# A row-wise logsumexp kernel: the bias of the first units as three one-row matmuls, and exp(bias) of the later stages made when they begin

## Chip, cores, metric

One core of a Trainium2 chip. The metric is the device time of one execution in microseconds (us), median of several executions; the profile page shows one of them. The profile's *span* is shorter than this time by about 1.8 us for the kernel before; that difference becomes part of the story.

## The reference

```python
def reference(x, bias):                    # x: 8 x 2048 x 2048 f32, bias: 8 x 256
    B, S, D = x.shape
    H = bias.shape[0]
    Dh = D // H
    x_heads = x.reshape(B, S, H, Dh).transpose(0, 2, 1, 3)
    x_heads = x_heads + bias[None, :, None, :]
    x_tiled = np.repeat(x_heads, 2, axis=2)
    mx = x_tiled.max(axis=-1, keepdims=True)
    return (mx.squeeze(-1) + np.log(np.exp(x_tiled - mx).sum(axis=-1))).astype(np.float32)
```

So 134 MB are read, and for each of 131,072 groups of 256 numbers one logarithm of a sum of exponentials is written twice.

## The kernel before

The rows are worked on in 64 units of 256 rows (2.097 MB each), in nine buffers `xt`. Units 0 to 53 are of one kind: PE adds the bias to heads 0 to 2 in PSUM (a bias matmul, then x times the identity), ACT takes exp; head 3 has exp on ACT and is multiplied by exp(bias) on DVE; heads 4 to 7 get the bias added on POOL, then exp on ACT; DVE sums heads 1 to 7, and ACT sums head 0 while it takes its exp. The last ten units use other divisions, which need more factors exp(bias). The parts that the change touches:

```python
    # bias as three bf16 parts that sum to the f32 value: made in one partition ...
    nc.gpsimd.tensor_copy(bparts[:, 0], bp)
    nc.gpsimd.tensor_sub(brest[:, 0], bp, bparts[:, 0])
    ...
    nc.gpsimd.tensor_copy(bparts[:, 2], brest[:, 1])
    # ... and gathered into three partitions, so that one matmul with 3 rows of ones adds all three
    for i in range(3):
        nc.gpsimd.dma_start(out=b3[i : i + 1, :], in_=bparts[:, i])
    ...
    for i, c in enumerate(range(G0, D, MM)):          # bias of heads 4 to 7, in all partitions
        spread(ps[i], c, c + MM)
        nc.vector.tensor_copy(b_rep[:, c - G0 : c - G0 + MM], ps[i])
    for c in range(W0, W2, MM):                       # factors exp(bias) of heads 3 to 6
        spread(w_ps[:, c - W0 : c - W0 + MM], c, c + MM)
    nc.scalar.activation(out=w_ps, in_=w_ps, func=ACT.Exp)
    nc.scalar.activation(out=w_sb, in_=b_rep[:, W1 - G0 :], func=ACT.Exp)
    ...
            for h, p in enumerate(got):               # the bias matmuls of one unit
                nc.tensor.matmul(p, lhsT=ones3, rhs=each_row(b3, h * Dh, Dh, K),
                                 start=True, stop=False)
    ...
            def pool_part(t=t, ...):                  # after a unit's sums: its buffer is loaded anew
                if add:
                    later(m, t, k0, k1, sums, add)
                if k1 == K and t + NBUF < T:
                    load(t + NBUF)
```

The softmax here doesn't subtract the row's maximum and nothing guards it: scores larger than these inputs give would overflow.

Of the kernel before, what the change touches and what calls it, by code (L numbers as in the profile page):

```python
# [11 lines left out]
ACT = mybir.ActivationFunctionType  # L12
# [2 lines left out]

K = 2
NBUF = 9

NWARM = 3

# [29 lines left out]
def kernel(  # L50
# [6 lines left out]
    nc = tc.nc  # L57
    P = nc.NUM_PARTITIONS
    B, S, D = x.shape
    H, Dh = bias.shape  # L60
# [5 lines left out]
    MM = 512  # L66


    V0, W0, G0, W1, W2 = Dh, 3 * Dh, 4 * Dh, 6 * Dh, 7 * Dh
# [7 lines left out]
    b_rep = sb.tile([P, D - G0], F32, name="b_rep")  # L77
    w_sb = sb.tile([P, D - W1], F32, name="w_sb")
    ident = sb.tile([P, P], F32, name="ident")
    ones = sb.tile([1, P], F32, name="ones")  # L80
    ones3 = sb.tile([3, P], BF16, name="ones3")
    b3 = sb.tile([3, CPE], BF16, name="b3")
    bparts = sb.tile([1, 3, CPE], BF16, name="bparts")
# [5 lines left out]
    res_last = sb.tile([P, P, 2], F32, name="res_last")  # L89
    xts = [sb.tile([P, K, D], F32, name=f"xt{i}") for i in range(NBUF)]  # L90
    w_ps = pp.tile([P, W2 - W0], F32, name="w_ps")


    one_ps = pp.tile([P, MM], F32, name="one_ps")
# [5 lines left out]
    def modes_of(t):  # L100
        return [modes for t0, modes in STAGES if t0 <= t][-1]

    def pieces(t):

        if len(modes_of(t)) == 1:
            return [(0, K, 0, D)]
        cols = [[(0, D)]] * K if t < T - 1 else LAST_COLS
        return [(k, k + 1, c0, c1) for k in range(K) for c0, c1 in cols[k]]

    def rows_of(t):  # L110

        b, blk = divmod(t, NBLK)
        v = x[b, blk * P * K : (blk + 1) * P * K, :]
        if b < B - 1:
            return v.rearrange("(p k) d -> p k d", k=K)
        return v.rearrange("(k p) d -> p k d", k=K)
# [5 lines left out]
    def on_x(t, ins, after):  # L122
        known = [u for u in users[t] if u.ins.engine != ins.ins.engine]
        for before in range(t % NBUF, t, NBUF):
            known += users[before]
# [12 lines left out]
    def load(t):  # L138
        after = last_uses[t - NBUF] if t >= NBUF else []
        for k0, k1, c0, c1 in pieces(t):  # L140
            loads[t, k0, c0] = on_x(
                t,
                nc.sync.dma_start(
                    out=xts[t % NBUF][:, k0:k1, c0:c1],
                    in_=rows_of(t)[:, k0:k1, c0:c1],
                ),
                after,
            )
# [14 lines left out]
    nc.scalar.dma_start(out=brow, in_=bias.rearrange("h j -> (h j)").unsqueeze(0))  # L163
    for t in range(NBUF):
        load(t)
# [9 lines left out]
    nc.gpsimd.tensor_sub(brest[:, 1], brest[:, 0], bparts[:, 1])  # L175
    nc.gpsimd.tensor_copy(bparts[:, 2], brest[:, 1])
    for i in range(3):
        nc.gpsimd.dma_start(out=b3[i : i + 1, :], in_=bparts[:, i])


    def spread(dst, c0, c1):
        nc.tensor.matmul(
            dst, lhsT=ones, rhs=brow[:, c0:c1], start=True, stop=True
        )

    for i, c in enumerate(range(G0, D, MM)):
        spread(ps[i], c, c + MM)
        nc.vector.tensor_copy(b_rep[:, c - G0 : c - G0 + MM], ps[i])
    for c in range(W0, W2, MM):
        spread(w_ps[:, c - W0 : c - W0 + MM], c, c + MM)  # L190
    nc.scalar.activation(out=w_ps, in_=w_ps, func=ACT.Exp)
    nc.scalar.activation(out=w_sb, in_=b_rep[:, W1 - G0 :], func=ACT.Exp)


    n_ps = [0]
# [4 lines left out]
    def on_bank(i, ins):  # L200
        for j, u in bank_users[i // 2]:
            if j != i and u.ins.engine != ins.ins.engine:
                tc.declare_no_dep(ins.ins, u.ins, reason="another bank")
        bank_users[i // 2].append((i, ins))
        return ins

    def put_bias(m, k0, k1):



        if m["late"]:
            pair = pairs[n_ps[0] % 2]
            n_ps[0] += 1
            got = [one_ps, pair[:, 0:MM], pair[:, MM : 2 * MM]]
            for h, p in enumerate(got):
                nc.tensor.matmul(  # L216
                    p,
                    lhsT=ones3,
                    rhs=each_row(b3, h * Dh, Dh, K),
                    start=True,  # L220
                    stop=False,
                )
            return got + [pair]
        n = m["pe"] * Dh
        rows = min(k1 - k0, max(MM // n, 1))
        got = []
        for k in range(k0, k1, rows):
            for c in range(0, n, MM):
                w = min(n - c, MM)
                bank = n_ps[0] % len(ps)  # L230
                p = ps[bank][:, 0 : rows * w]
                n_ps[0] += 1
                mm = nc.tensor.matmul(
                    p,
                    lhsT=ones3,
                    rhs=each_row(b3, c, w, rows),
                    start=True,
                    stop=False,
                )
                on_bank(bank, mm)  # L240
                got.append((k, k + rows, c, w, bank, p))
        return got

    def add_x(m, t, k0, c0, c1, got):
# [3 lines left out]
        for ka, kb, c, w, bank, p in got:  # L248
            if not c0 <= c < c1:
# [3 lines left out]
                lhsT=ident,  # L253
                rhs=xts[t % NBUF][:, ka:kb, c : c + w],
                start=False,
# [8 lines left out]
    def keep_warm():  # L264
        for _ in range(NWARM):
            nc.tensor.matmul(  # L266
                tps[B % 2][:, 0], lhsT=ident, rhs=ident, start=True, stop=True
            )
# [45 lines left out]
    def each_row(src, c, n, k_rows):  # L314

        return bass.AP(
            tensor=src.tensor,
            offset=src.offset + c,
            ap=[src.ap[0], [0, k_rows], [1, n]],
        )  # L320
# [124 lines left out]
    def sums_of(t):  # L445

        b, blk = divmod(t, NBLK)
        if b < B - 1:
            return R[b][:, :, :, blk]
        return R_last[:, :, blk, :].rearrange("p h k -> p k h")  # L450
# [20 lines left out]
    for t in range(T):  # L471
        xt = xts[t % NBUF]
        sums = sums_of(t)
        for k0, k1, c0, c1 in pieces(t):
            m = modes_of(t)[k0]
            add = None
            heads = []
            if c0 == 0:
                bias_here = bias_there
            if m["late"]:  # L480
                pe_part = late_heads(m, t, bias_here, sums)
            else:
                heads = add_x(m, t, k0, c0, c1, bias_here)

                def pe_part(t=t, heads=heads, sums=sums):
                    for k, h, bank, p, mm in heads:
                        sum_biased(t, k, h, bank, p, mm, sums)

            if c0 == 0:
                if next_units and not m["late"]:  # L490
                    bias_there = put_bias(*next_units.pop(0))
                if t > T_PROMPT and m["g0"] == H:
                    keep_warm()
                if m["g0"] < H:
                    add = g_add(m, t, k0, k1)
                if t < T - 1 or k0 == 0:
                    flush(for_pool)
            if t == T_PROMPT and c0 == 0:
                spread(one_ps, V0, W0)
                nc.scalar.activation(out=one_ps, in_=one_ps, func=ACT.Exp)  # L500
            h0 = max(c0 // Dh, m["pe"])
            h1 = min(c1 // Dh, m["g0"])
            hf = max(h0, min(h1, H - m["fold"]))
            if h0 < h1 and not m["late"]:
                done = exp_inplace(
                    t, xt[:, k0:k1, h0 * Dh : h1 * Dh], loads[t, k0, c0]
                )
                if hf < h1:
                    for_pool.append(fold(t, k0, hf, h1, sums, done))
            if c0 == 0:  # L510
                flush(for_pe)
            if not m["late"]:
                for k in range(k0, k1):
                    for h in range(h0, hf):
                        weigh(
                            t,
                            xt[:, k, h * Dh : (h + 1) * Dh],
                            h,
                            sums[:, k, h : h + 1],
                            done,  # L520
                        )

            def pool_part(t=t, m=m, k0=k0, k1=k1, sums=sums, add=add):
# [5 lines that stand above are left out]
            for_pool.append(pool_part)  # L529
            if m["g0"] < H:  # L530
                pe_part()
                if m["late"]:
                    bias_there = put_bias(*next_units.pop(0))
            elif heads:
                for_pe.append(pe_part)

        fb, at = divmod(t - 2, NBLK)
        if fb >= 0 and at == NBLK - 1:
            finish(fb)
            if fb == B - 2:  # L540
                store()
# [35 lines left out]
```

## Time and profile before

| | before |
|---|---|
| time, median (range) | 326.98 us (326.78 to 327.11) |
| span of the profiled run (its own time) | 325.4 us (327.16 us) |
| HBM read and written | 134.23 MB + 1.05 MB |

The page's views are quoted in the prediction below. How to read them: the slice rows are tenths of busy time in 40 equal slices; the chain follows the last instruction back to what released it; a timeline row is start, length, engine, line, what, with what ended the idle time in brackets.

### The profile page before, as it was taken

The numbers are of one execution on the slowest core, as the hardware profiler recorded it, in microseconds if no ns is written. First come the engines' busy times: TensorE is split into PE (matmuls) and PEld (weight loads), VectorE is DVE, ScalarE is ACT, GpSimd is POOL, SyncE is SP. The second block draws the span as 40 slices with busy tenths as digits, with TensorE's granted clock in tenths as the row PEclk, the third lists the DMA queues.
The fourth block names the chain that finished last, engine by engine and source line by source line (L and its number), as shares of the span: only waits on it lengthen the run. The fifth ranks groups of instructions, "written<-read, shape, count | busy, mean of one in ns | idle before, by whom it ended". The sixth has DMA issues, their size and how long they took to land.

```text
span 325.4 us, 2350 instructions
## 1 busy us (share of the span) xinstructions
PE 263.2 (81%) x649; PEld 98.6 (30%) x649; DVE 284.0 (87%) x306; ACT 264.7 (81%) x425; POOL 290.7 (89%) x123
## 2 busy tenths in 40 slices
PE   5398999599888789779779788887877897399984
PEld 2033333233323223223223223323223332044442
DVE  1008999999999999998998899989899799999985
ACT  1139999499969878987887969698788778889995
POOL 7999999899999999999999999999999899958874
PEclk9999999899979987997997979798998989569999
DMA  7999999999999999999999999999999999999995
GB/s 293 428 435 429 427 433 422 425 433 429 427 427 431 425 424 433 425 425 434 426 425 431 431 422 427 429 429 427 431 427 426 429 425 429 415 421 421 424 394 154
DMA packets 11934, 135.42 MB, mean 416 GB/s; under 512 B 1361, under 2 KB 1745, under 8 KB 2961
## 3 DMA queue, kind: packets, MB, share of 16 engines
q1 hardware_dynamic: 11824, 135.27, 98.9%
q8 instruction: 5, 0.08, 0.1%
q14 instruction: 7, 0.06, 0.0%
q0 software_dynamic: 96, 0.00, 0.0%
q10 hardware_dynamic: 2, 0.01, 0.0%
HBM read 134.23 MB, written 1.05 MB: 416 GB/s over the span
## 4 chain that ended last, share of the span: by engine, by line
DMA 48%; DVE 35%; POOL 6%; ACT 6%; PE 3%; issue 1%; SPq 0%; DVEq 0%
DMA xt<-in_x_dram 45%; DVE R L350 29%; ACT xt L331 5%; DVE xt L343 5%; POOL xt L325 4%; DMA b<-bparts 2%; PE pair L275 2%; DVE xt L366 2%; PE one_ps L275 1%; ACT xt L293 1%; DMA brow<-in_bias_dram 1%; POOL brest L173 1%; POOL brest L175 1%; PE pair L216 0%; POOL bparts L172 0%
## 5 line engine op out<-in xcount | busy, mean ns | idle before, releaser
L325 POOL TENSOR_TENSOR xt<-xt,b_rep 128x2048 f32<-128x2048 f32 x57 | 258.8, 4543 | 20.1 <-DMA xt<-in_x_dram 20.1
L350 DVE TENSOR_REDUCE R<-xt 128x14 f32<-128x3584 f32 (+1 forms) x56 | 214.5, 3831 | 1.9
L331 ACT ACTIVATE xt<-xt 128x2560 f32<-128x2560 f32 (+5 forms) x77 | 158.1, 2062 | 13.4 <-POOL xt L325 12.5
L275 PE MATMUL pair<-xt,ident 128*128 128x512 f32 x216 | 115.1, 660 | 0.0
L275 PE MATMUL one_ps<-xt,ident 128*128 128x512 f32 x108 | 66.7, 702 | 23.1 <-DMA xt<-in_x_dram 23.1
L293 ACT ACTIVATE xt<-pair 128x1024 f32<-128x1024 f32 x54 | 56.3, 1042 | 20.7 <-PE pair L275 19.3
L275 PEld LDWEIGHTS pair<-xt,ident 128*128 128x128 f32 x216 | 46.2, 214 | 61.5 <-issue 61.5
L343 DVE TENSOR_TENSOR xt<-xt,w_ps 128x512 f32<-128x512 f32 x54 | 36.8, 681 | 27.8 <-ACT xt L331 27.7
L286 ACT ACTIVATE xt<-one_ps 128x256 f32<-128x256 f32 x108 | 40.6, 391 | 7.9 <-PE one_ps L275 7.9
L216 PE MATMUL one_ps<-b,ones 3*128 3x512 bf16 x54 | 20.7, 383 | 18.4 <-ACT xt L286 12.4
L216 PEld LDWEIGHTS <-ones 3*128 3x128 bf16 x162 | 13.5, 92 | 70.2 <-issue 63.8
L216 PE MATMUL pair<-b,ones 3*128 3x512 bf16 x108 | 32.3, 378 | 0.0
L275 PEld LDWEIGHTS one_ps<-xt,ident 128*128 128x128 f32 x108 | 17.0, 198 | 46.4 <-DMA xt<-in_x_dram 39.6
L251 PE MATMUL pair<-xt,ident 128*128 128x512 f32 (+1 forms) x36 | 21.0, 669 | 7.2 <-DMA xt<-in_x_dram 7.1
L286 ACT ACTIVATION_READ_ACCUMULATOR xt<-one_ps 128x1 f32 x108 | 23.5, 218 | 0.0
L366 DVE CUSTOM_DVE_ANT_0 xt<-xt,w_ps 128x256 f32<-128x256 f32 x61 | 22.4, 419 | 0.0
L390 POOL TENSOR_TENSOR xt<-xt 128x128 f32<-128x128 f32 (+3 forms) x39 | 13.9, 356 | 3.1
L382 POOL TENSOR_TENSOR xt<-xt,w_sb 128x256 f32<-128x256 f32 (+1 forms) x13 | 10.1, 773 | 5.4 <-ACT xt L331 4.8
L266 PE MATMUL tpair<-ident 128*128 128x128 f32 x84 | 13.6, 300 | 0.5 <-ACT res L421 0.5
L306 ACT ACTIVATE xt<-pair 128x256 f32<-128x256 f32 x33 | 12.3, 387 | 0.0
L266 PEld LDWEIGHTS tpair<-ident 128*128 128x128 f32 x84 | 11.1, 200 | 4.1 <-issue 3.0
L366 DVE CUSTOM_DVE_ANT_0 xt<-xt,one_ps 128x256 f32<-128x256 f32 x27 | 10.6, 416 | 0.7 <-ACT xt L331 0.7
(40 smaller groups left out, 68.5 us busy)
## 6 DMA issues: line engine op xcount, KB each, us to landing
xt<-in_x_dram SPq DMA_DIRECT2D x57, 2048.0 KB, 30.8
xt<-in_x_dram SPq DMA_DIRECT2D x12, 1024.0 KB, 24.7
xt<-in_x_dram SPq DMA_DIRECT2D x4, 256.0 KB, 11.4
out_dram<-res SPq DMA_DIRECT2D x1, 896.0 KB, 6.6
xt<-in_x_dram SPq DMA_DIRECT2D x2, 384.0 KB, 16.0
xt<-in_x_dram SPq DMA_DIRECT2D x2, 128.0 KB, 6.3
out_dram<-res_last SPq DMA_DIRECT2D x1, 128.0 KB, 1.7
b<-bparts POOLq DMA_DIRECT2D x3, 1.5 KB, 6.4
```

What stands on the lines that cost most here:

```text
L216: nc.tensor.matmul(p, lhsT=ones3, rhs=each_row(b3, h * Dh, Dh, K), start=True, stop=False,)
L251: mm = nc.tensor.matmul(p, lhsT=ident, rhs=xts[t % NBUF][:, ka:kb, c : c + w], start=False, stop=True,)
L266: nc.tensor.matmul(tps[B % 2][:, 0], lhsT=ident, rhs=ident, start=True, stop=True)
L275: mm = nc.tensor.matmul(p, lhsT=ident, rhs=xts[t % NBUF][:, :, h * Dh : (h + 1) * Dh], start=False, stop=True,)
L286: act = nc.scalar.activation(out=xts[t % NBUF][:, k, 0:Dh], in_=got[0][:, k * Dh : (k + 1) * Dh], func=ACT.Exp, accum_out=sums[:, k, 0:1],)
L293: act = nc.scalar.activation(out=xts[t % NBUF][:, :, Dh : m["pe"] * Dh].rearrange("p k (h j) -> p h k j", j=Dh), in_=got[-1].rearrange("p ...
L325: add = nc.gpsimd.tensor_tensor(out=v, in0=v, in1=each_row(b_rep, c - G0, D - c, k1 - k0), op=ALU.add)
L331: return on_x(t, nc.scalar.activation(out=v, in_=v, func=ACT.Exp), [after])
L343: mul = nc.vector.tensor_tensor(out=f, in0=f, in1=each_row(w_ps, m["pe"] * Dh - W0, n, k1 - k0), op=ALU.mult,)
L350: red = nc.vector.tensor_reduce(out=sums[:, k0:k1, h0:H], in_=v.rearrange("p k (h j) -> p k h j", j=Dh), op=ALU.add, axis=mybir.AxisListTy ...
L366: ttr = nc.vector.tensor_tensor_reduce(out=v, in0=v, in1=w, scale=1.0, scalar=0.0, op0=ALU.mult, op1=ALU.add, accum_out=dst,)
L390: done = nc.gpsimd.tensor_tensor(out=v[:, :, 0:n], in0=v[:, :, 0:n], in1=v[:, :, n : 2 * n], op=ALU.add)
```

## The change

Its intent: the first unit waits for three small transfers (the gathering of `b3`) and for factors that nobody needs before the last ten units. So the first five units take the parts where they are made, in one partition, as three matmuls of one row each; the transfers go out from ACT's queue; and only head 3's factor is made at the start, the others when the later stages begin.

```diff
-        nc.gpsimd.dma_start(out=b3[i : i + 1, :], in_=bparts[:, i])
+        nc.scalar.dma_start(out=b3[i : i + 1, :], in_=bparts[:, i])
...
-    for c in range(W0, W2, MM):
-        spread(w_ps[:, c - W0 : c - W0 + MM], c, c + MM)
-    nc.scalar.activation(out=w_ps, in_=w_ps, func=ACT.Exp)
-    nc.scalar.activation(out=w_sb, in_=b_rep[:, W1 - G0 :], func=ACT.Exp)
+    w_late = w_ps[:, 0 : G0 - W0]
+    spread(w_late, W0, G0)
+    nc.scalar.activation(out=w_late, in_=w_late, func=ACT.Exp)
+
+    def prompt_factors():
+        spread(one_ps, V0, W0)
+        nc.scalar.activation(out=one_ps, in_=one_ps, func=ACT.Exp)
+        nc.scalar.activation(
+            out=w_ps[:, G0 - W0 :], in_=b_rep[:, 0 : W2 - G0], func=ACT.Exp
+        )
+        nc.scalar.activation(out=w_sb, in_=b_rep[:, W1 - G0 :], func=ACT.Exp)
...
+            parts = [(ones3, b3)]
+            if n_ps[0] <= NEARLY:                     # NEARLY = 5
+                parts = [(ones3[0:1], bparts[:, i]) for i in range(3)]
             for h, p in enumerate(got):
-                nc.tensor.matmul(p, lhsT=ones3, rhs=each_row(b3, ...), start=True, stop=False)
+                for i, (lhsT, b) in enumerate(parts):
+                    nc.tensor.matmul(p, lhsT=lhsT, rhs=each_row(b, ...), start=i == 0, stop=False)
...
             if t == T_PROMPT and c0 == 0:
-                spread(one_ps, V0, W0)
-                nc.scalar.activation(out=one_ps, in_=one_ps, func=ACT.Exp)
+                prompt_factors()
```

More of the change, by code (lines that the diff above doesn't have):

```diff
@@ L17 @@
 NBUF = 9
+NEARLY = 5
 NWARM = 3
@@ L214, in put_bias @@
             got = [one_ps, pair[:, 0:MM], pair[:, MM : 2 * MM]]
+            parts = [(ones3, b3)]
+            if n_ps[0] <= NEARLY:
+                parts = [(ones3[0:1], bparts[:, i]) for i in range(3)]
             for h, p in enumerate(got):
-                nc.tensor.matmul(
-                    p,
-                    lhsT=ones3,
-                    rhs=each_row(b3, h * Dh, Dh, K),
-                    start=True,
-                    stop=False,
-                )
+                for i, (lhsT, b) in enumerate(parts):
+                    nc.tensor.matmul(
+                        p,
+                        lhsT=lhsT,
+                        rhs=each_row(b, h * Dh, Dh, K),
+                        start=i == 0,
+                        stop=False,
+                    )
             return got + [pair]
```

## The prediction

> **What bounds the kernel now.** I first read the engine table and the row of DMA, because five engines are near 80 to 90% busy and none is full, so a share of busy time cannot name the bound.
>
> ```profile
> PE 263.2 (81%) x649; PEld 98.6 (30%) x649; DVE 284.0 (87%) x306; ACT 264.7 (81%) x425; POOL 290.7 (89%) x123
> DMA  7999999999999999999999999999999999999995
> GB/s 293 428 435 429 427 433 422 425 433 429 427 427 431 425 424 433 425 425 434 426 425 431 431 422 427 429 429 427 431 427 426 429 425 429 415 421 421 424 394 154
> ```
>
> The transfers are full in every slice but the first and the last. A unit is 128x4096 f32 = 2.097 MB. The stage table gives 427 GB/s with a DMA share of 1.01 for 5 to 315 us:
>
> ```profile
> 5.00:315.00 310.00, 255.18 (x619) 94.77 (x619) 276.91 (x266) 256.32 (x404) 282.43 (x106) 0.92 1.01 427
> ```
>
> So a unit takes 2.097 / 0.427 = 4.91 us to load, and there are 64. Next I read the chain that ended last, which runs through DVE early and DMA late:
>
> ```profile
> 9.66 7.13 DMA b<-bparts
> ...
> 25.86 0.70 DVE xt L343
> 26.58 3.89 DVE R L350
> ...
> 120.84 30.73 DMA xt<-in_x_dram
> ...
> 294.48 20.15 DMA xt<-in_x_dram
> 314.63 0.02 issue
> ```
>
> The trap is here. The chain says that the wait for the bias rows (7.13 us) and the late start of DVE are on the path. But the chain follows one release backward: buffer free, so load issued, so load landed. It does not show the other loads ahead in the queue, which have to land first anyway. To see whether the queue ever ran dry I read the load issues in order of time:
>
> ```profile
> 0.74 3.73 SPq L143 DMA_DIRECT2D xt<-in_x_dram  x7
> 8.52 0.80 SPq L143 DMA_DIRECT2D xt<-in_x_dram  x2
> 30.55 9.34 SPq L143 DMA_DIRECT2D xt<-in_x_dram  x3
> ```
>
> (They come from several windows; the rows in between cut the same groups.) SP could issue the eighth load when load 0 had landed, at 8.52 us. Load 8 therefore lands near 8.52 + 8 x 4.91 = 47.8 us. The next load needs the buffer of unit 0 and was issued at 30.55 us. At that moment 47.8 - 30.55 = 17.2 us of transfers, 3.5 units, were still queued. That is the smallest stock of the run: DVE then needs 3.89 + 0.60 + 0.02 = 4.51 us per unit, less than the 4.91 us of a load, so the stock grows by 0.4 us per unit until DVE has caught up, which the chain shows near 120 us. The late start has been paid for out of the nine buffers; it cost the transfers nothing.
>
> Thus the time is: 8.52 us to the first landing, then 306.1 us until the second half of unit 62 has landed at 314.63 (62 x 4.91 = 304.4, plus the lower rate of 415 to 394 GB/s that the GB/s row shows for the last, smaller pieces), then a tail of 325.37 - 314.63 = 10.7 us. The measured 326.98 is 1.6 us above the span.
>
> **What the Trainium skill says.** "DMA: Bandwidth & Descriptors", section "Specifications", names a fabric ceiling of 435 GB/s. The trace agrees: 427 over 310 us, 435 in the best full slices. The same table's 358 GB/s for HBM per core does not fit this trace, which exceeds it throughout; the measurement decides. The same page, "Queues, rings and completion order", says that the engines alternate between the rows that have work, packet by packet; so three tiny transfers moved to ACT's row should land within microseconds even with loads queued. The bias row, issued by ACT, took 1.74 us in the chain, though with the loads only starting. "TensorE: Matmul & The Clock Gate", Part 1, gives 426.7 ns start to start for 512 columns cold and 215.7 ns warm; the trace has a triple of bias matmuls in 18.29 - 16.93 = 1.36 us cold (0.45 each) and 27.34 - 26.61 = 0.73 us later (0.24 each), so it agrees with some overhead. "ScalarE: Activation LUTs", section "What ACT_TABLE_LOAD costs", gives 186 ns + 0.833 ns per column for an ACTIVATE; the 128x1024 and 128x512 exp of the bias took 1.01 and 0.62 us against 1.04 and 0.61, so 128x768 should take 0.83 us.
>
> **The change part by part.**
>
> 1. The first five units no longer wait for the rows of b to be gathered.
>
> ```profile
> 7.34 3.62 PE L182 MATMUL w_ps<-brow,ones 1*128 1x512 f32 x4
> 16.93 0.58 PE L216 MATMUL one_ps<-b,ones 3*128 3x512 bf16 x1 [5.97 <-DMA b<-bparts]
> ```
>
> The last part is ready at 8.55 us (cast at 7.74, 0.81 long). PE now does 256 instead of 1024 columns of spreading there: about 3.62 / 4 = 0.9 us, to 8.4. Then nine one-row matmuls, 9 x 0.45 = 4.1 us cold, to about 12.5, and the six f32 passes of unit 0, about 3.0 us warm (23.22 to 26.06 for unit 1) to 4.3 us half cold: 15.5 to 17. Before they ended at 22.5. POOL, rid of 1.64 us of issuing, starts its first add near 8.6 and ends near 13.2, before it is needed. So the DVE's first work moves from 25.86 to 19 to 20.5 us: 5.5 to 7 us earlier.
>
> 2. These five units cost PE 6 more matmuls each, 6 x 0.24 = 1.5 us warm. A unit is then 9 x 0.24 + 3.0 = 5.2 us on PE, slower than DVE's 4.51. Over the four steps after unit 0 this gives back up to 4 x (5.2 - 4.51) = 2.8 us. At unit 5 DVE is ahead by some 3 to 4 us instead of 6. It then catches up with the loads some 3.5 / 0.4 = 9 units sooner: the DVE stretch of the chain should end near 70 to 90 us instead of 120. From there every load, every buffer and every engine stands as it stood before. Effect on the landing of unit 62: zero.
>
> 3. The three b rows go out on ACT's queue. In the order of the instructions they also take three of the eight completion semaphores that SP's loads rotate through: load 4 now waits for load 0, load 6 for load 1, loads 7 to 9 for the three b rows. Four loads are in flight at first instead of seven. Four loads are 4 x 4.91 = 19.6 us of transfer, and the next follows at the first landing, 8.5 us: no gap. The b rows are issued near 9 to 10 us; even if they took 7 us as before, loads 2 to 6 cover until about 8.52 + 6 x 4.91 = 38 us.
>
> 4. ACT makes 128x768 and 128x512 of exp(bias) at the start of the mixed stage, 0.83 + 0.61 less overlap of about 0.1 = 1.3 us, and no longer 1.5 us at 11 us, where it was idle. What lies there:
>
> ```profile
> 277.05 0.58 ACT L500 ACTIVATE one_ps<-one_ps 128x512 f32<-128x512 f32 x1 [0.35 <-PE one_ps L182]
> 284.17 3.29 ACT L331 ACTIVATE xt<-xt 128x2048 f32<-128x2048 f32 x2 [0.51 <-POOL xt L325]
> 289.12 4.66 ACT L331 ACTIVATE xt<-xt 128x2048 f32<-128x2048 f32 x3 [0.94 <-POOL xt L325]
> ```
>
> The next two waits of ACT for POOL are 0.51 + 0.94 = 1.45 us, so 1.3 us is absorbed by 289 us. DVE is busy until 281.4 with unit 53 and has the operands for unit 54 before. If it were not absorbed, ACT's solid stretch from 289 to 309.4 us would carry a rest to where it meets the loads again at 309.6.
>
> Sum: start 0, loads 0, tail 0 (its order of work is unchanged), with perhaps +0 to +0.3 us from part 4. I predict the time of before, 326.9 us.
>
> **Rivals.** (a) The chain taken at its word: 6.5 us earlier start, or the 3 us left after five units, come off the end, giving 320 to 324 us. For it: the b row transfer is in the chain. Against it: 17 us of queued loads when the first buffer comes free, and a full DMA row in all middle slices. (b) The nine small matmuls make PE the bound early, or the new semaphore order starves the queue: 1 to 5 us lost, 328 to 332. Against it: five units at 5.2 us from an earlier start release every buffer no later than before, and four loads in flight outlast the wait. A b row held behind all queued loads would be needed. (c) The ACT work at the mixed stage reaches the tail in full: 328.2. Against it: the 1.45 us of waits behind it. (d) The program no longer issues DMA from POOL, which may shorten something outside the span; no view shows that, and at most some tenths of a us are plausible.
>
> **Range and chances.** The repeats of before span 326.78 to 327.11; a run on another occasion may differ by perhaps 0.3%. With rival (c) above and (a), (d) below I take 325.9 to 328.0. The 2% border is 6.5 us: below 320.4 the transfers would have to be faster than 427 GB/s, which nothing in the change does; above 333.5 needs an empty queue. Faster 0.01, same 0.98, slower 0.01.
>
> **What would show it.** Right: the first bias matmul near 8.5 us, nine of them, first DVE reduce near 20 us, first reissued load near 24 us, the DMA row still full with the same GB/s, DVE's stretch in the chain ending sooner, the last large landing at 314.5 +- 0.5, tail 10.7 us. Wrong: GB/s of the middle slices moved (then the transfers depend on what engines do beside them), a dip of DMA in the first 50 us (part 3), or an ACT or DVE wait after 290 us that was not there (part 4).

## The result, and the profile after

| | before | after |
|---|---|---|
| time, median (range), 4 runs each | 326.88 us (326.63 to 327.11) | 327.45 us (327.32 to 327.88) |
| span of the profiled run | 325.4 us | 325.7 us |

The ratio is 1.002, with a 95% interval of 1.0003 to 1.0037. (A ratio is the mean time of one kernel's fast runs over that of the other's fast runs of the same rounds, so it is not quite the ratio of the medians quoted.) The time is the same within 2%, inside the stated range, and a little *longer*, not shorter.

First the page of the changed kernel, busy times and slices:

```profile
PE 271.1 (83%) x677; PEld 101.8 (31%) x677; DVE 284.5 (87%) x306; ACT 264.1 (81%) x426; POOL 289.2 (89%) x120
DMA  7999999999999999999999999999999999999994
GB/s 297 429 431 427 435 423 426 433 429 427 427 435 425 423 434 427 427 433 424 429 428 425 430 427 431 425 431 431 427 425 428 429 429 426 417 422 424 416 396 136
```

The DMA row is as full as before, slice by slice, at the same rates; only PE has more to do. Next the start in order of time (several windows, rows chosen). Of the kernel before, the DVE's first and fifth unit:

```profile
25.86 0.69 DVE L343 TENSOR_TENSOR xt<-xt,w_ps 128x512 f32<-128x512 f32 x1 [17.59 <-ACT xt L331]
...
43.93 0.68 DVE L343 TENSOR_TENSOR xt<-xt,w_ps 128x512 f32<-128x512 f32 x1
```

Of the changed kernel, the bias matmuls, the first exp on ACT, and the DVE's first, fifth and sixth unit:

```profile
9.20 1.48 PE L231 MATMUL one_ps<-bparts,ones 1*128 1x512 bf16 x3
10.48 2.76 PE L231 MATMUL pair<-bparts,ones 1*128 1x512 bf16 x6
15.29 0.38 ACT L301 ACTIVATE xt<-one_ps 128x256 f32<-128x256 f32 x1 [4.76 <-PE one_ps L290]
...
21.53 0.69 DVE L358 TENSOR_TENSOR xt<-xt,w_ps 128x512 f32<-128x512 f32 x1 [12.24 <-ACT xt L346]
...
45.83 0.69 DVE L358 TENSOR_TENSOR xt<-xt,w_ps 128x512 f32<-128x512 f32 x1 [1.90 <-ACT xt L346]
...
50.36 0.68 DVE L358 TENSOR_TENSOR xt<-xt,w_ps 128x512 f32<-128x512 f32 x1
```

The intent is met at unit 0: DVE begins it at 21.53 us instead of 25.86. But DVE begins unit 4 at 45.83 and unit 5 at 50.36, against 43.93 and 48.45 before (each step there is some 4.5 us). The head start of 4.3 us has become a lag of 1.9 us. The table of stages says why; here is the stretch from 20 to 45 us, first of the kernel before, then of the changed one. The columns after the stretch are its length, busy us of PE, PEld, DVE, ACT and POOL, the granted PE clock, the DMA share and GB/s.

```profile
20.00:45.00 25.00, 23.27 (x58) 8.70 (x57) 18.97 (x10) 23.26 (x37) 23.81 (x6) 1.00 1.01 429
```

```profile
20.00:45.00 25.00, 25.00 (x60) 8.91 (x59) 18.30 (x8) 16.91 (x25) 23.19 (x6) 0.80 1.00 429
```

With nine bias matmuls per unit PE is busy without a pause, and its granted clock is 0.80 instead of 1.00 as a mean of this stretch (0.80 and 0.81 in the two further runs with nine buffers and these matmuls, e4 and e2 below; 1.00 in e1 and e3 without them). It is not a steady 0.80: taken by 2 us, the clock is 0.50 from 22 to 24 and from 28 to 30 us, and 1.00 from 32 to 38. So a unit takes (45.83 - 21.53) / 4 = 6.1 us, not the 5.2 of the prediction. Step by step, the clock was 0.97 in the one that took 4.93 us (PE at it from 31 to 36 us) and 0.74 to 0.75 in the three that took 6.35 to 6.51. None of this reaches the transfers: 429 GB/s in both.

The chain of the changed kernel has DVE catching up later in this run, not sooner, and shows how the kernel ends:

```profile
145.89 3.90 DVE R L365
149.79 0.02 SPq L145
149.84 31.24 DMA xt<-in_x_dram
...
315.07 1.60 ACT xt L346
316.67 0.02 issue
316.69 0.42 DVE xt L381
```

The DVE stretch ends at 149.8 us (before: 120.8). The tail begins with DVE at 316.69 (before: after the landing at 314.63 and an exp of 1.71, at 316.38). At the mixed stage ACT has the new work and, in this run, no waits behind it:

```profile
278.54 0.58 ACT L198 ACTIVATE one_ps<-one_ps 128x512 f32<-128x512 f32 x1 [1.17 <-PE one_ps L185]
279.03 0.81 ACT L199 ACTIVATE w_ps<-b_rep 128x768 f32<-128x768 f32 x1
279.76 0.62 ACT L202 ACTIVATE w_sb<-b_rep 128x512 f32<-128x512 f32 x1
```

In the chain, ACT is then solid from here to 316.67. So two questions stood open: is the start really free because of the stock of queued loads (and not for another reason), and where do the 0.57 us come from?

### The profile page after: what moved, and what is told of

Its sections match the earlier page's. It is cut to its first block, busy times and chain, and to the rows that moved or that the text cites. A ratio compares the mean times of both kernels' runs of the same rounds, so it can differ in the third digit from the quotient of the medians.

```text
span 325.7 us, 2403 instructions
## 1 busy us (share of the span) xinstructions
PE 271.1 (83%) x677; PEld 101.8 (31%) x677; DVE 284.5 (87%) x306; ACT 264.1 (81%) x426; POOL 289.2 (89%) x120
## 4 chain that ended last, share of the span: by engine, by line
DVE 36%; DMA 30%; PE 16%; ACT 15%; POOL 1%; issue 0%; SPq 0%; ACTq 0%; DVEq 0%
DVE R L365 30%; DMA xt<-in_x_dram 29%; ACT xt L346 10%; PE pair L290 6%; DVE xt L358 5%; PE one_ps L290 3%; ACT xt L321 3%; PE pair L231 2%; DVE xt L381 2%; POOL xt L340 1%; PE one_ps L231 1%; PE pair L185 1%; ACT xt L308 1%; DMA brow<-in_bias_dram 1%; PE one_ps L185 0%
## 5 line engine op out<-in xcount | busy, mean ns | idle before, releaser
L290 PE MATMUL pair<-xt,ident 128*128 128x512 f32 x216 | 117.4, 672 | 0.0
L290 PE MATMUL one_ps<-xt,ident 128*128 128x512 f32 x108 | 66.2, 697 | 23.3 <-DMA xt<-in_x_dram 23.3
L308 ACT ACTIVATE xt<-pair 128x1024 f32<-128x1024 f32 x54 | 55.8, 1034 | 24.9 <-PE pair L290 23.3
L231 PEld LDWEIGHTS <-ones 3*128 3x128 bf16 (+1 forms) x192 | 16.6, 94 | 67.0 <-issue 56.9
L290 PEld LDWEIGHTS one_ps<-xt,ident 128*128 128x128 f32 x108 | 16.9, 196 | 46.6 <-DMA xt<-in_x_dram 38.6
L231 PE MATMUL pair<-b,ones 3*128 3x512 bf16 x98 | 28.9, 374 | 0.0
L231 PE MATMUL one_ps<-b,ones 3*128 3x512 bf16 x49 | 18.7, 381 | 10.4 <-ACT xt L301 10.4
L301 ACT ACTIVATION_READ_ACCUMULATOR xt<-one_ps 128x1 f32 x108 | 22.7, 210 | 0.0
L281 PE MATMUL tpair<-ident 128*128 128x128 f32 x84 | 14.3, 312 | 1.7 <-ACT res L436 1.7
```

What stands on the lines that cost most here:

```text
L231: nc.tensor.matmul(p, lhsT=lhsT, rhs=each_row(b, h * Dh, Dh, K), start=i == 0, stop=False,)
L281: nc.tensor.matmul(tps[B % 2][:, 0], lhsT=ident, rhs=ident, start=True, stop=True)
L290: mm = nc.tensor.matmul(p, lhsT=ident, rhs=xts[t % NBUF][:, :, h * Dh : (h + 1) * Dh], start=False, stop=True,)
L301: act = nc.scalar.activation(out=xts[t % NBUF][:, k, 0:Dh], in_=got[0][:, k * Dh : (k + 1) * Dh], func=ACT.Exp, accum_out=sums[:, k, 0:1],)
L308: act = nc.scalar.activation(out=xts[t % NBUF][:, :, Dh : m["pe"] * Dh].rearrange("p k (h j) -> p h k j", j=Dh), in_=got[-1].rearrange("p ...
```

## The experiments

### One part of the change at a time

**The transfers from ACT's queue, alone (e1).**

```diff
-        nc.gpsimd.dma_start(out=b3[i : i + 1, :], in_=bparts[:, i])
+        nc.scalar.dma_start(out=b3[i : i + 1, :], in_=bparts[:, i])
```

> The kernel before with one part of the change alone: the three b rows are sent from ACT's queue instead of POOL's. Observed so far: the changed kernel is 0.57 us slower in the median (327.45 against 326.88) though its spans (325.2 to 325.7) hardly differ from the 325.4 of before, so its time lies 2.1 to 2.2 us above its span against 1.8 before. Theory Q (the extra lies outside the span and comes with the queue from which the b rows go): 327.2 to 327.5, time minus span about 2.15, span 325.2 to 325.4. Theory F (it comes from the 1.3 us of exp(bias) put on ACT at the mixed stage): 326.9, time minus span 1.8. Theory P (it comes from the nine small matmuls): 326.9. In every theory the first unit starts about as before, 15 to 17 us, since it still waits for the rows.

Measured: 326.84 us against 326.80, ratio 0.9999 (0.9987 to 1.0012). Time minus span is 1.77 to 1.86 in its five runs. So the queue costs nothing, and Q is out. The start was not as expected: in this run the rows were there sooner (first bias matmul at 14.12 us, before 16.93), and DVE ran thus in units 0, 4 and 5:

```profile
23.11 0.69 DVE L343 TENSOR_TENSOR xt<-xt,w_ps 128x512 f32<-128x512 f32 x1 [15.04 <-ACT xt L331]
...
41.18 0.68 DVE L343 TENSOR_TENSOR xt<-xt,w_ps 128x512 f32<-128x512 f32 x1
...
45.70 0.68 DVE L343 TENSOR_TENSOR xt<-xt,w_ps 128x512 f32<-128x512 f32 x1
```

With one line changed, and three bias matmuls per unit as before, unit 5 begins 4.7 us sooner than with the whole change (45.70 against 50.36), though unit 0 begins 1.6 us later. And all of it is worth nothing at the end.

**The nine one-row matmuls, alone (e2).**

```diff
+            parts = [(ones3, b3)]
+            if n_ps[0] <= NEARLY:
+                parts = [(ones3[0:1], bparts[:, i]) for i in range(3)]
```

(with the loop over `parts` of the change; transfers and factors as before)

> The kernel before with the nine one-row matmuls in the first five units alone; b rows from POOL and factors at the start, as before. Theory Q: 326.9, time minus span about 1.8. Theory F: 326.9. Theory P: 327.4. In all: first bias matmul moves ahead to about 11 us (w_ps spreads of 1024 columns still stand before it), DVE's first reduce to 23 to 25 us, DMA row full, no gain at the end.

Measured: 326.70 us against 326.80, ratio 0.9998 (0.9985 to 1.0012); time minus span 1.76 to 1.83. So P is out. The first bias matmul came at 11.53 us and DVE's first work at 24.31; unit 5 began 5 us after the kernel before (48.45 us), with a granted clock of 0.81 from 20 to 45 us:

```profile
53.54 0.68 DVE L351 TENSOR_TENSOR xt<-xt,w_ps 128x512 f32<-128x512 f32 x1
```

A start that is worse by 5 us from unit 5 on costs nothing either.

**The late factors, alone (e3).** The change without the other two parts: transfers from POOL, NEARLY = 0.

```diff
-NEARLY = 5
+NEARLY = 0
-        nc.scalar.dma_start(out=b3[i : i + 1, :], in_=bparts[:, i])
+        nc.gpsimd.dma_start(out=b3[i : i + 1, :], in_=bparts[:, i])
```

(against the changed kernel)

> The kernel before with only the exp(bias) factors of the later stages made when those begin. Theory Q: 326.9, time minus span about 1.8. Theory F: span 0.2 to 0.4 longer, 327.2 to 327.4; ACT then has no wait between about 280 us and the tail, and the DVE stretch of the tail starts 0.2 to 0.4 us later than 316.38. My prediction said that two waits of 1.45 us would absorb the 1.3 us: then span 325.4 and 326.9.

Measured: 327.26 us against 326.80, ratio 1.0017 (1.0004 to 1.0029). The extra is here. But its profile shows ACT as the prediction had it:

```profile
276.83 0.58 ACT L198 ACTIVATE one_ps<-one_ps 128x512 f32<-128x512 f32 x1 [0.36 <-PE one_ps L185]
277.35 0.81 ACT L199 ACTIVATE w_ps<-b_rep 128x768 f32<-128x768 f32 x1
278.10 0.61 ACT L202 ACTIVATE w_sb<-b_rep 128x512 f32<-128x512 f32 x1
...
288.90 4.66 ACT L346 ACTIVATE xt<-xt 128x2048 f32<-128x2048 f32 x3 [0.29 <-POOL xt L340]
```

Before, ACT waited for POOL 0.51 us at 284 and 0.94 us at 289; here 0.29 us are left, so the waits took up the new work, and ACT meets POOL again at 289 us. The spans of the five runs are 324.9, 325.9, 325.0, 325.2 and 325.1, those of the kernel before in the same job 324.8 to 325.2. Time minus span is 2.11 to 2.20 instead of 1.73 to 1.85. So theory F, in the form "ACT's work reaches the tail", is out too; the extra lies outside the span, as Q had said, but comes with the factors and not with the queue. None of the three theories had it whole.

**The whole change once more (e4).**

> The changed kernel once more, beside its three parts on the same chip. All theories: 327.3 to 327.6, ratio 1.001 to 1.0025. If it is now within 0.2 us of before, the difference first seen was noise between runs and none of Q, F, P is needed.

Measured: 327.14 us, ratio 1.0011 (0.9999 to 1.0024), a touch below what was expected. Spans 324.9 to 325.3, like the kernel before; time minus span 2.12 to 2.19. Its profile has ACT waiting 0.34 us for POOL at 288.85: the solid stretch of the first profile was not there. In that first run ACT came to the mixed stage 1.5 us later than before (278.54 against 277.05), after PE had worked from 270 to 275 us at a granted clock of 0.66, and nothing was left to take up the factors; its span of 325.7 is the longest of the changed kernel's nine. That explanation of the one run rests on its trace and was not tested by itself. The DVE stretch ended at 122.4 us here, so the 149.8 was also one run's; how little this point says is seen in e5 below, which starts like the kernel before (120.8) and has it at 89.8.

### Where the 0.35 us outside the span come from

**One ACT instruction more, nothing late (e5).**

```diff
-    nc.scalar.activation(out=w_ps, in_=w_ps, func=ACT.Exp)
+    nc.scalar.activation(out=w_ps[:, 0:256], in_=w_ps[:, 0:256], func=ACT.Exp)
+    nc.scalar.activation(out=w_ps[:, 256:], in_=w_ps[:, 256:], func=ACT.Exp)
```

> The kernel before with the exp of w_ps cut in two instructions (256 and 768 columns), both still at the start: one ACT instruction more, as in e3_late_factors, but nothing late. The extra of e3_late_factors lies outside the span (2.1 to 2.2 us between time and span, 1.8 in the kernel before, e1 and e2). Theory N (one ACT instruction more, or the way the program lies in memory): 327.15, time minus span 2.15. Theory L (it comes from exp work placed in the middle of the program): 326.8, time minus span 1.8.

Measured: 326.86 us against 326.89, time minus span 1.75 to 1.86. Theory N is out for one instruction more on ACT.

**One factor late (e6).**

```diff
-    nc.scalar.activation(out=w_sb, in_=b_rep[:, W1 - G0 :], func=ACT.Exp)
...
                 nc.scalar.activation(out=one_ps, in_=one_ps, func=ACT.Exp)
+                nc.scalar.activation(out=w_sb, in_=b_rep[:, W1 - G0 :], func=ACT.Exp)
```

> The kernel before with only the exp of w_sb (128x512, 0.6 us of ACT) moved to the mixed stage; as many ACT instructions as before. The late factors as a whole added 0.35 us between time and span (2.15 against 1.8) and nothing to the span. Theory L (any exp of the factors placed in the middle adds it): 327.15, 2.15 between time and span. Theory W (it comes with the other part, the shorter spread on PE and the exp of w_ps from b_rep): 326.85, 1.8.

Measured: 326.74 us against 326.81, time minus span 1.74 to 1.84. An exp moved to the middle does not bring it: L is out.

**The other factor late (e7).** The late factors as above, but

```diff
+    nc.scalar.activation(out=w_sb, in_=b_rep[:, W1 - G0 :], func=ACT.Exp)
     def prompt_factors():
...
-        nc.scalar.activation(out=w_sb, in_=b_rep[:, W1 - G0 :], func=ACT.Exp)
```

> The complement of e6_one_late: the shorter spread of w_ps and its late exp from b_rep as in the change, w_sb at the start as before. Theory L: 327.15, time minus span 2.15. Theory W: 327.15 too, 2.15. If both e6 and e7 stay at 1.8 it takes both together; if e6 has it and e7 has not, it is w_sb's place alone.

Measured: 327.18 us against 326.81, ratio 1.0011 (0.9998 to 1.0023), spans 325.0 to 325.2, time minus span 2.10 to 2.18. The ratio alone would not settle it, since its interval takes in 1; the time minus span does. So it is W: the extra comes with the part that spreads 256 instead of 1024 columns of `w_ps` and makes the rest from `b_rep`. (Its two halves, the shorter spread at the start and the late exp, were not run apart.) The separation is clean in every run, though spans are recorded to 0.1 us only:

| kernels | time minus span, all their runs |
|---|---|
| before (27 runs), e1, e2, e5, e6, d10, d25, n5_before, n5_act_queue | 1.73 to 1.86 us |
| changed, e3, e4, e7, n5_after | 2.10 to 2.20 us |

Why a kernel with that part takes 0.35 us more before the first or after the last recorded instruction, no view of the profile shows: it stays open.

### Is the start free because of the stock of loads?

**A later start, nine buffers (d10, d25).** Useless exp on ACT before the first unit, 19 or 35 of them:

```diff
+    for _ in range(19):
+        nc.scalar.activation(
+            out=res[:, 0:2].rearrange("q b p k r -> q (b p k r)"),
+            in_=b_rep[0 : H * NBLK, :],
+            func=ACT.Exp,
+        )
```

> The kernel before, nine buffers, with ACT kept busy by 19 useless exp of 64x1024 (about 0.94 us each, 18 us in all) before the first unit, so that unit 0 is ready about 10 us later: DVE's first reduce near 36.5 us, the buffer of unit 0 free near 40.5. Theory S (stock): load 8 lands near 47.8, so 7 us of loads are still queued; the DMA row stays full and the time is 326.9, within 0.3. Theory C (the chain at its word: a later start of DVE is paid at the end): 336 to 337. Theory C is the mirror of the rival in the prediction that gave 320 to 324 for an earlier start.

Measured: 327.03 us against 326.81, ratio 1.0011 (0.9994 to 1.0028). One exp took 1.09 us from start to start, so the delay was somewhat longer than planned:

```profile
37.73 0.69 DVE L350 TENSOR_TENSOR xt<-xt,w_ps 128x512 f32<-128x512 f32 x1 [28.68 <-ACT xt L338]
```

DVE begins 37.73 - 25.86 = 11.9 us later and the time rises by 0.2 us, which is not clear of noise. Its DMA row is full:

```profile
DMA  7999999999999999999999999999999999999995
GB/s 295 434 427 429 435 425 424 427 431 429 421 433 429 425 425 432 421 428 433 420 431 429 427 427 422 433 425 425 435 426 421 431 429 425 416 421 421 420 398 164
```

Theory C, the chain at its word, wanted 336 to 337. It is out.

> The same with 35 useless exp (about 33 us), unit 0 ready about 25 us later, its buffer free near 55.5 us, after the last queued load has landed at 47.8. Theory S: the transfers stand still once, for 55.5 + 1.5 - 47.8 = 9 us by the arithmetic, 12 to 13 us if the restart costs as much more as it did with five buffers (7.3 us lost against 3.9 expected); time 336 to 341, with a dip of the DMA row near 48 to 60 us. Theory C: 351 to 352. Rival H (the start never matters): 326.9.

Measured: 344.58 us, ratio 1.054 (1.0524 to 1.0556). The DMA and GB/s rows now show the queue run dry; a slice is 8.6 us:

```profile
DMA  8999940899999999999999999999999999999995
GB/s 302 428 431 431 429 178 0 276 383 397 429 429 431 427 427 429 427 421 429 431 426 427 427 435 435 422 427 429 426 427 433 427 423 427 418 422 424 418 397 154
```

The stage table has 274 GB/s for 44 to 48 us and 0 for 52 to 60: the transfers stop about when load 8 was reckoned to land (47.8 us), and start again when SP issues the next load at 59.87 us, after unit 0. So the arithmetic of the stock names the place of the gap. The time is 3.6 us above the upper end of what S expected. One reason is that the delay was 29.3 us (DVE at 55.18) and not 25, so that the standstill lasts from about 47 to 60 us. The other is a slow restart: SP issues the next loads one at a time, at 59.87, 66.91, 71.43 and 75.94 us, each as DVE gives a buffer back, and the rate is 254 to 397 GB/s until 80 us. Together this accounts for the whole rise: from 24 to 100 us the mean is 326 GB/s against 428 before, 76 x (1 - 326 / 428) = 18.1 us of transfers. Of 29.3 us of delay 17.8 arrive at the end; of 11.9 us, 0.2.

**Five buffers instead of nine: kernel before, ACT's queue alone, whole change.** (The last two units have buffers of their own in all three.)

```diff
-NBUF = 9
+NBUF = 5
+    def buf(t):
+        return t % NBUF if t < T - 2 else NBUF + t - (T - 2)
```

> The kernel before with five x buffers instead of nine (the last two units have buffers of their own, for the check). Theory S (stock: the late start is paid for out of the loaded units that queue up): load 4 lands near 8.5 + 4 x 4.91 = 28.2 us, the buffer of unit 0 comes free at 30.5, the next bytes flow some 1.5 us later, so the transfers stand still once for 3.9 us and the time is 330.7 us, +-0.7. Rival H (the start is hidden whatever the buffers): 326.8. Rival B (five buffers are too few all along): 335 or more.

> Five buffers, b rows from ACT's queue only, nothing else of the change. With nine buffers this kernel ended unit 0 at 27.7 us. Theory S: a gap of 27.7 + 1.5 - 28.2 = 1.0 us, then none; time 327.9, +-0.7, so 2.8 us faster than n5_before. Rival H: 326.8, no difference. Rival B: 335 or more for both.

> Five buffers and the whole change. With nine buffers the changed kernel freed units 0 to 5 at about 26.1, 32.6, 39.0, 43.9, 50.4, 54.9 us, while load 4 lands at 28.1. Theory S: no gap for load 5, then 0.9, 1.5, 0 and 1.6 us, 4.0 in sum, time about 331.0 with the 0.3 us that the late factors add, so no better than n5_before, though its first unit is ready 4 us sooner. A reader who goes by the first unit alone expects no gap at all and 327.0 to 327.3. Rival H: 327.2.

Measured: 338.69 us (338.28 to 340.97), 335.78 (335.70 to 336.10) and 336.93 (334.15 to 337.50), each against 326.89 of the kernel before with nine. All three are in the region that I had given to rival B; but B said "all along", and the slices say otherwise. GB/s of the three in that order (slices of 8.4 us):

```profile
GB/s 299 427 430 175 405 420 432 423 425 434 432 428 421 432 429 428 421 428 431 431 419 430 434 427 418 434 432 430 419 430 433 425 425 420 423 423 420 412 275 16
```

```profile
GB/s 295 428 438 186 379 431 432 428 430 430 426 428 430 430 423 430 424 430 431 424 432 429 426 426 429 428 430 430 426 430 429 424 426 423 420 422 421 418 374 29
```

```profile
GB/s 294 434 432 367 303 340 363 393 430 430 430 432 428 424 430 427 426 428 431 426 424 431 428 428 425 432 428 422 434 428 425 428 428 420 422 421 423 403 388 46
```

The loss is once, near 25 to 34 us, in the first two, and from 25 to 68 us in the third, where nine matmuls hold up each of the first five units. From 70 to 280 us five buffers carry 427 to 429 GB/s. What the start cost can be read from the stage table: from 24 to 68 us the means are 374, 375 and 356 GB/s against 428 with nine buffers, so 44 x (1 - 374 / 428) = 5.6, 5.4 and 7.4 us of transfers were lost. A second reading is where ACT waits for the first half of unit 62 to land, at 312.09 us with nine buffers, and here, in the same order:

```profile
319.38 1.70 ACT L334 ACTIVATE xt<-xt 128x1792 f32<-128x1792 f32 x1 [2.20 <-DMA xt<-in_x_dram]
```

```profile
319.59 1.70 ACT L334 ACTIVATE xt<-xt 128x1792 f32<-128x1792 f32 x1 [2.22 <-DMA xt<-in_x_dram]
```

```profile
322.06 1.70 ACT L349 ACTIVATE xt<-xt 128x1792 f32<-128x1792 f32 x1 [0.67 <-DMA xt<-in_x_dram]
```

These are 7.3, 7.5 and 10.0 us later, but not all of it is the start's: with five buffers the 896 KB of results `res`, some 2.1 us of transfer, are issued at 300.9, 301.1 and 304.7 us, before this half lands, and at 315.4 us, after it, with nine. So the start cost 5.6, 5.4 and 7.4 us, where S expected 3.9, 1.0 and 4.0. The mechanism holds, the sizes do not: a restart cost more than the 1.5 us that I had put in, and in this run the b rows came late from ACT's queue as well (DVE began at 25.25 us; 23.11 in the run with nine). The third against the first, one profile each: the whole change, which begins unit 0 at 20.94 instead of 25.63 us, loses 1.8 us *more* of transfer time. The total times order otherwise (336.93 against 338.69 us). The tails differ: in the profile of the first, PE ran at a granted clock of about 0.5 from 324 to 332 us; that this is the reason was not tested, and I draw nothing from those differences.

No version meant to beat both kernels was run: what moves the start by a few us lies behind the same 47 us of queued loads.

## Why the prediction was right, point by point

**The verdict.** 326.9 was predicted, 327.45 measured, inside 325.9 to 328.0; "within 2%" was given 0.98. The mechanism is shown, not only argued: a start 11.9 us later costs 0.2 us or nothing (d10), one 5 us later from unit 5 on costs nothing (e2), one 2.8 us earlier gains nothing (e1), and the same start costs 5 to 7 us of transfer time once the stock is cut to five buffers. Rival (a), the chain at its word, is refuted by the first and the third of these.

**Bound and stock.** "That is the smallest stock of the run", 17.2 us: right in kind. In the changed kernel the first buffer is free at 26.22 us with some 21 us queued (load 8 lands near 8.44 + 8 x 4.91 = 47.7), but the smallest stock moved to unit 4, free at 50.44: 47.7 + 4 x 4.91 - 50.44 = 16.9 us. That it is nearly the same is chance: a larger stock at unit 0 was used up by the slower units after it.

**Part 1, first unit.** The failing number is DVE's start: 19 to 20.5 us predicted, 21.53 measured. The bias row landed 1.0 us later than before (2.76 us in the chain, 1.74 before); that is no effect of the change, since it took 1.54 to 2.76 us in the profiles, and up to 2.67 us in kernels with the start of before. And the six f32 passes were all slow: from 13.18 to 18.2, 5.0 us, where I had 3.0 to 4.3 and where the same six take 2.8 us from 23.2 us on before. (The clock column says 1.00 in this stretch too; that they were "cold" is read from their durations alone.) The first load issued anew followed at 26.22 us, where 24 was named.

**Part 2, five units.** The term mis-sized is "9 x 0.24 + 3.0 = 5.2 us on PE"; it measured 6.1, at a mean granted clock of 0.80. I had taken the warm duration for granted; in the step with a clock of 0.97 the term was about right (4.93 us). So "At unit 5 DVE is ahead by some 3 to 4 us" was wrong even in sign (1.9 us behind), and so was the stretch of DVE "near 70 to 90 us" (149.8 and 122.4). Wrong with it is the point against rival (b), that these units "release every buffer no later than before": unit 4's came free at 50.44 us, 1.9 us later. The sum was safe only because this step does not reach the end.

**Part 3, the loads' semaphores.** Right: SP issued four loads, two more at 8.44 us, the rest after, and the second to fifth slices have 427 to 435 GB/s. The b rows took 5.5 us to land (6.4 before): microseconds, as said. Over all profiles it was 5.5 to 5.8 us from ACT's queue (five) and 5.9 to 6.6 from POOL's (nine), a difference that did not matter here.

**Part 4, the factors.** The 128x768 exp took 0.81 us, 0.83 predicted. "1.3 us is absorbed by 289 us": shown in the late-factors run and in the repeat (0.29 and 0.34 us of waiting left). In the first profile they were not, and its span is 0.3 us above the profile of before.

**What was missed.** 0.35 us between time and span, clean in every run of every kernel with the `w_ps` part. That the sum allowed "+0 to +0.3 us" from part 4 is luck: it was meant for ACT's work reaching the tail, and the extra does not come that way. (The prediction's "1.6 us above the span" sets the median of other executions against the span of the profiled one; against its own time it is 1.8.) Rival (d) looked outside the span, but for a gain and for another reason. The cause of the 0.35 us is open.

## What to carry to other kernels

When the chain that ended last runs through a load, ask how many loads stood in the queue before it: a late start is free as long as each buffer comes back before the last load queued by then has landed. Here 17 us were in hand; 11.9 us of delay were free and 29.3 were not, and nothing between was run. Before shortening a start, compare that stock with the delay, or lengthen the start by a dose and see whether the time moves. And look at the unit at which the head start is to be used, not at the first one: six more matmuls per unit turned 4.3 us gained at unit 0 into 1.9 us lost at unit 5.

## What the Trainium skill lacked or had wrong

- "DMA: Bandwidth & Descriptors", section "Specifications": the table gives 358 GB/s for HBM per core without saying when it holds. This one core has 427 GB/s over 310 us, and the prediction took the row to be wrong for it. The same page, section "Bandwidth", has the answer: 358 is each core's part when both cores of a pair stream, and it measured 425 for one alone, which fits here, as the fabric ceiling of 435 does. What does not fit is that section's remark that for transfers from HBM the 358 binds.
- "TensorE: Matmul & The Clock Gate", Part 1: it has activity lift the throttle and idle time bring it back. Here the stretch from 20 to 45 us had a granted clock of 1.00 with PE busy 23.3 of 25 us, and 0.80 (a mean of times at 0.50 and at 1.00) with PE busy all 25 us by the profile, when nine bias matmuls instead of three stood in each unit. The page does not lead one to expect this; what in the added matmuls does it, no run here separates.
- No page has it: a difference between the device time and the profile's span that is steady for a kernel, 1.73 to 1.86 us for some and 2.10 to 2.20 us for others, and moves with one small part of the program.
